# One load of nine tiles in place of a load of two and a load of seven, at the start of a fused LoRA kernel

## The chip, the cores and the metric

The kernel runs on one core of a Trainium2 chip. The metric is device time in microseconds of one execution. A core has a matrix engine (TensorE, "PE" in the profile), a vector engine (VectorE, "DVE"), an activation engine (ScalarE, "ACT"), a general engine (GpSimd, "POOL") and a sequencing engine (SyncE, "SP"). Sixteen DMA engines move data between the chip's memory (HBM) and the on-chip memory (SBUF). The engines run side by side and meet at semaphores. In this kernel every DMA is issued by SP, on one queue.

## The reference

```python
def setup_inputs():
    batch, seq, d_model, r = 16, 512, 768, 16
    # x (16, 512, 768), A (768, 16) * 0.1, B (16, 768) * 0.1, all float32; scale = 0.5

def reference(x, A, B, scale):
    lora = np.matmul(np.matmul(x, A), B)
    return (x + scale * lora).astype(np.float32)
```

So every token, a row of 768 floats, gets a low-rank correction added: y = x A has 16 numbers per token, and out = x + 0.5 y B. There are 16 * 512 = 8192 tokens. x and out are 25.2 MB each.

## The kernel before, in words

**Tiles, parts and groups.** A tile is 128 tokens, one on each SBUF partition, so there are 64 tiles of 128 x 768 floats (384 KB each). The tiles are cut twice, by two different sizes. For the transfers there are five parts of 9, 7, 16, 16 and 16 tiles (`PARTS`); within a part each partition holds that many neighbouring tokens, so a load of n tiles reads one contiguous row of n * 3 KB for each partition. `LOADS` lists the loads as (part, first tile, number of tiles), `STORES` the stores. For the computation there are eight groups of eight tiles (`GROUP`). x stays in SBUF in float32 (`x_all`, called x_sb in the profile), the correction is added in place, and the stores read from there. There is room for 48 tiles. The last part's 16 tiles therefore go where parts 0 and 1 were, and its two loads wait until the stores of these parts are done.

**One group.** Half of the eight tiles are narrowed to float16 (xn) by ScalarE and half by GpSimd (`narrowed`, L194). VectorE transposes them in 32 x 32 blocks (xt, L250). TensorE multiplies them with A, spread out as a block-diagonal weight w_bd, in 24 matmuls (y_ps, L281). ScalarE copies the result, scaled, into the block-diagonal y_bd (four instructions, L238). TensorE multiplies that with B, four pairs of tiles one after another, each pair into one of two halves of PSUM (lora_ps, L302). VectorE adds each pair to x in place (L255). In VectorE's order the transposes of group g + 1 stand ahead of the four additions of group g.

**Group 0 and the weights** have an order of their own. GpSimd clears its buffers, builds `pick`, narrows the first two tiles of x (L194, called with 0, 0, 2), then narrows B (L212) when it has landed, then builds w_bd from A transposed (L214, L220). ScalarE narrows tiles 2 and 3, then 4 to 7. VectorE first transposes A (L243), then the two halves of group 0 (L250). GpSimd's narrowing of the first two tiles and the three loads of A count on the same semaphore, s_a, and VectorE's transpose of A waits for all four. A narrowing waits for the load that its tiles come with: `load_of` looks that up in `LOADS`, so the first narrowing on each engine that needs a load waits for all of that load.

**SP's queue.** The order is written out by hand: load 0, load 1, the three loads of A (after GpSimd has cleared a_rows), the load of B, loads 2 to 5; then, when group 1's additions are done and TensorE has finished the tenth pair of tiles (`s_lora` at 2 * PAIRS + 2), the stores of parts 0 and 1; when each of these has landed, a load of the last part (L139); then the stores of parts 2, 3 and 4 (L149), each after the group that completes it, the first of them not before TensorE has begun the pairs of group 5 (`s_raise` at 6). SP does nothing but issue and wait, and the sixteen DMA engines work their own lists of rows off in the order of issue: each of them gets 8 of the 128 rows of a load or store.

Of the kernel before, what the change touches and what calls it, by code (L numbers as in the profile page):

```python
# [28 lines left out]
def kernel(  # L29
# [66 lines left out]
    def memory(t2, i, s, n):  # L96
        S = PARTS[i]
        return t2[ds(parts[i], S * P), :].rearrange("(p s) d -> p s d", s=S)[:, ds(s, n), :]

    def held(i, s, n):  # L100
        return tiles(where.index((i, s)), n)

    def tiles(t, n):
        return x_all[:, ds(t % ROOM, n), :]

    LOADS = [
        (0, 0, 2), (0, 2, 7), (1, 0, 7), (2, 0, 8), (2, 8, 8), (3, 0, 16), (4, 0, 8), (4, 8, 8)
    ]
    s_load = [sem(f"s_load{k}") for k in range(len(LOADS))]

# [25 lines left out]
    def on_sync(e):  # L136
        def load(k):
            ld = LOADS[k]
            e.dma_start(out=held(*ld), in_=memory(x2, *ld)).then_inc(s_load[k], 16)  # L139

        def summed(k):
            e.wait_ge(s_sum, sorted(set(STORED)).index(STORED[k]) + 1)
            if STORED[k] + 1 < NG:

                e.sem_inc(s_free[PAIRS - 1], 1)

        def store(k, done):
            st = STORES[k]
            e.dma_start(out=memory(out2, *st), in_=held(*st)).then_inc(done, 16)  # L149

        load(0)
        load(1)
        e.wait_ge(s_ready, 1)
        blocks = A.rearrange("(c e) r -> c (e r)", e=64)
        for c in range(SETS):
            e.dma_start(
                out=a_rows[c : SET * SET : SET, :], in_=blocks[ds(c * SET, SET), :]
            ).then_inc(s_a, 16)
        e.wait_ge(s_brows, 1)
        e.dma_start(out=b_rows[0 : R * APART : APART, :], in_=B).then_inc(s_b, 16)  # L160
        for k in range(2, len(LOADS) - 2):
            load(k)

        for p in range(2, PAIRS):
            e.sem_inc(s_free[p], 1)
        summed(0)


        e.wait_ge(s_lora, 2 * PAIRS + 2)
        store(0, s_out0)  # L170
        store(1, s_out1)
        e.wait_ge(s_out0, 16)
        load(len(LOADS) - 2)
        e.wait_ge(s_out1, 16)
        load(len(LOADS) - 1)
        for k in range(2, len(STORES)):
            summed(k)
            if k == 2:


                e.wait_ge(s_raise, 6)
            store(k, s_out)
# [90 lines left out]
    def on_tensor(e):  # L273
# [58 lines left out]
        for p in range(PAIRS):  # L332
            raised(p)

    on_sync(nc.sync)
    on_gpsimd(nc.gpsimd)
    on_scalar(nc.scalar)
# [46 lines left out]
```

## Time and profile before

| | us |
|---|---|
| time, median of 3 runs | 123.75 (123.57 to 123.76) |
| time of the profiled execution | 123.43 |
| its span, first to last instruction | 121.6 |
| busy: VectorE | 81.7 |
| busy: TensorE matmuls | 49.8 |
| busy: ScalarE | 37.4 |
| busy: GpSimd | 28.4 |
| DMA packets' time, share of 16 engines over the span | 97.0% |

The page gives, for the slowest core, each engine's busy time, a strip of 40 slices with a digit for the busy tenths of each, the DMA queues, the chain of work that ended last, the costliest groups of instructions, and the DMA issues. The trace behind it answers with instructions in order of time, with what each waited for. It also has a record of each DMA packet: here one packet is one row of a load or store, with start, length and bytes. "Landing" of a DMA is the moment at which its semaphore has its full count.

### The profile page before, as it was taken

The numbers are of one execution on the slowest core, as the hardware profiler recorded it, in microseconds if no ns is written. First come the engines' busy times: TensorE is split into PE (matmuls) and PEld (weight loads), VectorE is DVE, ScalarE is ACT, GpSimd is POOL, SyncE is SP. The second block draws the span as 40 slices with busy tenths as digits, with TensorE's granted clock in tenths as the row PEclk, the third lists the DMA queues.
The fourth block names the chain that finished last, engine by engine and source line by source line (L and its number), as shares of the span: only waits on it lengthen the run. The fifth ranks groups of instructions, "written<-read, shape, count | busy, mean of one in ns | idle before, by whom it ended". The sixth has DMA issues, their size and how long they took to land.

```text
span 121.6 us, 884 instructions
## 1 busy us (share of the span) xinstructions
PE 49.8 (41%) x322; PEld 29.2 (24%) x322; DVE 81.7 (67%) x42; ACT 37.4 (31%) x43; POOL 28.4 (23%) x24
## 2 busy tenths in 40 slices
PE   0000209487457547746745734774674320000000
PEld 0000006253223424424423322442442110000000
DVE  0000970599999999999999989999995990000000
ACT  4000967626408312735340093643004000000000
POOL 7730567126009002605300080620000000000000
PEclk9999999999999999999999999999999995555555
DMA  3999999999999897999999999998999899899890
GB/s 63 437 431 457 446 398 469 404 420 469 437 517 420 356 517 336 427 421 410 446 416 436 428 428 485 420 517 372 404 517 404 372 517 404 372 517 404 372 517 0
DMA packets 1928, 50.43 MB, mean 415 GB/s; under 512 B 236, under 2 KB 236, under 8 KB 392
## 3 DMA queue, kind: packets, MB, share of 16 engines
q1 hardware_dynamic: 1928, 50.43, 97.0%
HBM read 25.26 MB, written 25.17 MB: 415 GB/s over the span
## 4 chain that ended last, share of the span: by engine, by line
DVE 33%; DMA 29%; PE 9%; ACT 6%; POOL 2%; issue 2%; SPq 0%; DVEq 0%
DVE x_sb L255 21%; DMA x_sb<-in_x_dram 20%; DVE xt L250 12%; DMA out_dram<-x_sb 9%; PE ps_yt L281 6%; ACT xn L194 3%; PE lora_ps L302 3%; ACT y_bd L238 2%; POOL xn L194 2%; SPq L139 0%; SPq L379 0%; DVEq L268 0%; SPq L134 0%
## 5 line engine op out<-in xcount | busy, mean ns | idle before, releaser
L255 DVE TENSOR_TENSOR x_sb<-x_sb,lora_ps 128x1536 f32<-128x1536 f32 x32 | 53.7, 1735 | 1.4 <-PE lora_ps L302 1.4
L194 ACT CAST xn<-x_sb 128x3072 f16<-128x3072 f32 (+1 forms) x9 | 23.4, 2609 | 35.9 <-DMA x_sb<-in_x_dram 24.8
L302 PE MATMUL lora_ps<-b_mm,y_bd 128*128 128x512 f16 (+1 forms) x128 | 25.0, 328 | 22.6 <-ACT y_bd L238 14.3
L194 POOL CAST xn<-x_sb 128x3072 f16<-128x3072 f32 (+1 forms) x8 | 20.7, 2586 | 43.9 <-DMA x_sb<-in_x_dram 24.6
L250 DVE STREAM_TRANSPOSE xt<-xn 128x3072 f32<-128x3072 f32 (+1 forms) x9 | 27.1, 3006 | 5.3 <-PE ps_yt L281 4.4
L281 PE MATMUL ps_yt<-xt,w_bd 128*128 128x256 f16 x192 | 25.2, 282 | 12.2 <-DVE xt L250 12.2
L281 PEld LDWEIGHTS ps_yt<-xt,w_bd 128*128 128x128 f16 x192 | 18.5, 99 | 19.7 <-issue 15.4
L302 PEld LDWEIGHTS lora_ps<-b_mm,y_bd 128*128 128x128 f16 x128 | 10.6, 97 | 35.5 <-ACT y_bd L238 16.6
L238 ACT ACTIVATE y_bd<-ps_yt 32x256 f16<-32x256 f32 x32 | 12.0, 374 | 18.7 <-PE ps_yt L281 18.4
L243 DVE STREAM_TRANSPOSE a_t<-a_rows 32x1024 f32<-32x1024 f32 x1 | 2.0, 1955 | 12.2 <-DMA a_rows<-in_A_dram 12.2
L315 PE MATMUL lora_ps<-b_half,pick 128*128 128x512 f16 (+1 forms) x2 | 0.8, 500 | 13.5 <-POOL b_half L212 13.5
L315 PEld LDWEIGHTS lora_ps<-b_half,pick 128*128 128x128 f16 x2 | 0.1, 105 | 13.5 <-issue 13.5
L212 POOL CAST b_half<-b_rows 128x768 f16<-128x768 f32 x1 | 0.8, 827 | 5.5 <-DMA b_rows<-in_B_dram 5.5
L220 POOL COPY w_bd<-w_one 32x384 f16<-32x384 f16 x4 | 2.0, 500 | 0.2
L194 ACT ACT_TABLE_LOAD x1 | 1.3, 1283 | 0.9 <-SPq L134 0.9
L202 POOL MEMSET w_bd<- 128x1536 f32 x1 | 1.4, 1372 | 0.0
L214 POOL CAST w_one<-a_t 32x384 f16<-32x384 f32 x1 | 0.9, 857 | 0.9 <-DVE a_t L243 0.9
L199 POOL MEMSET a_rows<- 32x1024 f32 x1 | 0.9, 941 | 0.5 <-SPq L134 0.5
L231 ACT CAST b_mm<-lora_ps 128x768 f16<-128x768 f32 x1 | 0.8, 798 | 0.0
L200 POOL MEMSET b_rows<- 128x768 f32 x1 | 0.7, 728 | 0.0
L203 POOL MEMSET y_bd<- 128x512 f32 x1 | 0.5, 514 | 0.0
L205 POOL TENSOR_SCALAR_AFFINE_SELECT pick<-pick 128x128 f16<-128x128 f16 x1 | 0.3, 298 | 0.0
(5 smaller groups left out, 0.6 us busy)
## 6 DMA issues: line engine op xcount, KB each, us to landing
out_dram<-x_sb SPq DMA_DIRECT2D x3, 6144.0 KB, 20.1
x_sb<-in_x_dram SPq DMA_DIRECT2D x4, 3072.0 KB, 17.6
x_sb<-in_x_dram SPq DMA_DIRECT2D x1, 6144.0 KB, 41.6
x_sb<-in_x_dram SPq DMA_DIRECT2D x2, 2688.0 KB, 12.4
out_dram<-x_sb SPq DMA_DIRECT2D x1, 3456.0 KB, 11.5
out_dram<-x_sb SPq DMA_DIRECT2D x1, 2688.0 KB, 17.7
x_sb<-in_x_dram SPq DMA_DIRECT2D x1, 768.0 KB, 4.5
a_rows<-in_A_dram SPq DMA_DIRECT2D x3, 16.0 KB
```

The source lines that it names most:

```text
L194: ins = copy(out=xn[:, ds(first, n), :], in_=tiles(t, n))
L199: e.memset(a_rows[0:Q], 0.0).then_inc(s_ready, 1)
L202: e.memset(w_bd.rearrange("p c k m -> p (c k m)").bitcast(fp32), 0.0)
L214: e.tensor_copy(out=w_one.rearrange("i (c e) k r -> i c e (k r)", c=SETS), in_=a_t[0:Q].rearrange("i k r (e c) -> i c e (k r)", c=SET)[:, ...
L220: e.tensor_copy(out=w_bd[ds(b * Q, Q), :, :, ds(b * Q, R)], in_=w_one).then_inc(s_w, 1)
L238: last = e.mul(out=y_bd[q, :, q], in_=y_ps[q, :, :], mul=sc)
L243: e.transpose(out=a_t[0:Q].rearrange("i k r c -> i (k r) c"), in_=a_rows[0:Q].rearrange("c (i k r) -> c (k r) i", k=2, r=R),).then_inc(s_r ...
L250: return e.transpose(out=ts[0], in_=ts[1])
L255: ins = e.tensor_tensor(out=xs, in0=xs, in1=lora[p % 2], op=mybir.AluOpType.add)
L281: mm = e.matmul(y_ps, w_bd[:, c, k, :], xv[:, :, c, :, k], start=(m == 0), stop=(m == MMS - 1),)
L302: mms.append(e.matmul(t[:, k, ds(n0, w)], y_bd[:, 2 * p + k, :], b_mm[:, ds(n0, w)], start=True, stop=True,))
L315: last = e.matmul(lora[0][:, 0, ds(n0, w)], pick.rearrange("p b r -> p (b r)"), b_half[:, ds(n0, w)], start=True, stop=True,)
```

## The change

The first nine tiles of x are one part in memory. They came as two loads, one of tiles 0 and 1 (rows of 6 KB) and one of tiles 2 to 8 (rows of 21 KB). Now they come as one load of nine tiles with rows of 27 KB, and SP issues one DMA fewer. The later loads keep their place in SP's order, with numbers one lower. The narrowings look up their load in the list: GpSimd's narrowing of tiles 0 and 1 now waits for the load of nine tiles, as ScalarE's of tiles 2 and 3 does (before, that waited for the load of seven). No instruction of the other engines is added, removed or reordered.

```diff
     LOADS = [
-        (0, 0, 2), (0, 2, 7), (1, 0, 7), (2, 0, 8), (2, 8, 8), (3, 0, 16), (4, 0, 8), (4, 8, 8)
+        (0, 0, 9), (1, 0, 7), (2, 0, 8), (2, 8, 8), (3, 0, 16), (4, 0, 8), (4, 8, 8)
     ]
...
         load(0)
-        load(1)
         e.wait_ge(s_ready, 1)
...
-        for k in range(2, len(LOADS) - 2):
+        for k in range(1, len(LOADS) - 2):
             load(k)
```

## The prediction

> **What bounds the kernel now.** I read the page's strip and queue table first, to see which resource is full, then the busy time by stretches, then the instructions of the start in order of time, then the chain up to the first store.
>
> ```profile
> span 121.6 us, 884 instructions
> ...
> DMA  3999999999999897999999999998999899899890
> ...
> q1 hardware_dynamic: 1928, 50.43, 97.0%
> ```
>
> No compute engine is over 67%, but the sixteen DMA engines are busy 97% of the span: 50.43 MB, nearly all of it x in and out. The strip dips only around slices 13 to 15, where loads give way to stores. So I cut the span there:
>
> ```profile
> core 0: us, PE busy (x) PEld busy (x) DVE busy (x) ACT busy (x) POOL busy (x), PEclk, DMA share, GB/s
> 1.97:12.10 10.13, 0.00 (x0) 0.00 (x0) 0.00 (x0) 0.22 (x1) 4.29 (x6) 1.00 1.04 414
> 12.10:44.45 32.35, 18.44 (x114) 10.84 (x114) 27.33 (x14) 17.67 (x18) 11.92 (x9) 1.00 1.01 432
> 44.45:46.45 2.00, 0.58 (x6) 0.53 (x7) 2.00 (x2) 0.00 (x0) 0.00 (x0) 1.00 0.91 393
> 46.45:47.30 0.85, 0.85 (x9) 0.55 (x6) 0.85 (x2) 0.00 (x0) 0.00 (x0) 1.00 1.22 521
> 47.30:62.50 15.20, 8.99 (x61) 5.31 (x60) 15.20 (x10) 8.27 (x10) 5.49 (x2) 1.00 1.00 427
> ...
> 77.00:120.25 43.25, 12.64 (x82) 6.91 (x79) 22.24 (x13) 5.73 (x9) 2.75 (x1) 0.76 0.97 418
> ```
>
> The last but one column is the DMA share (packets are counted by their start, so a short stretch can read over or under 1). It stays at 1: 0.91 and 1.22 together make up 1.00 over 44.45 to 47.30. The packet records say it row by row: from the first row at 1.98 to the last row's end at 120.22, no engine pauses by 0.05 us between two rows. The kernel therefore ends when the DMA engines have worked off a fixed list of rows. A change moves the time if it makes the list shorter, or lets an engine run out of rows before SP issues the next.
>
> The start, in order of time:
>
> ```profile
> 5.57 1.46 POOL L194 CAST xn<-x_sb 128x1536 f16<-128x1536 f32 x1 [0.73 <-DMA x_sb<-in_x_dram]
> 12.12 4.13 ACT L194 CAST xn<-x_sb 128x1536 f16<-128x1536 f32 x2 [9.93 <-DMA x_sb<-in_x_dram]
> 12.23 1.96 DVE L243 STREAM_TRANSPOSE a_t<-a_rows 32x1024 f32<-32x1024 f32 x1 [12.23 <-DMA a_rows<-in_A_dram]
> 12.52 0.83 POOL L212 CAST b_half<-b_rows 128x768 f16<-128x768 f32 x1 [5.49 <-DMA b_rows<-in_B_dram]
> ...
> 14.12 1.72 DVE L250 STREAM_TRANSPOSE xt<-xn 128x1536 f32<-128x1536 f32 x1
> 14.25 0.86 POOL L214 CAST w_one<-a_t 32x384 f16<-32x384 f32 x1 [0.90 <-DVE a_t L243]
> 15.17 2.18 POOL L220 COPY w_bd<-w_one 32x384 f16<-32x384 f16 x4
> 16.27 0.80 ACT L231 CAST b_mm<-lora_ps 128x768 f16<-128x768 f32 x1
> 16.28 1.78 DVE L250 STREAM_TRANSPOSE xt<-xn 128x1536 f32<-128x1536 f32 x1 [0.44 <-ACT xn L194]
> 18.18 0.77 PEld L281 LDWEIGHTS ps_yt<-xt,w_bd 128*128 128x128 f16 x5 [4.57 <-issue]
> 18.21 1.01 PE L281 MATMUL ps_yt<-xt,w_bd 128*128 128x256 f16 x4 [3.92 <-DVE xt L250]
> ```
>
> GpSimd narrows its two tiles at 5.57, long before anything else can go on. At 12.1 the load of seven, A and B land nearly together, and then VectorE, GpSimd and ScalarE each have a queue of work before TensorE can begin at 18.21. And the chain to the first store:
>
> ```profile
> 42.95 1.49 PE lora_ps L302 x8
> 44.44 0.02 issue
> 44.45 11.48 DMA out_dram<-x_sb
> ```
>
> The first store is issued at 44.45, when TensorE's tenth pair is done. VectorE has no idle time between its transpose at 22.51 and that moment (52.28, 42.36, 32.44, 22.51: a period of 9.92 us), so a delay of group 0 arrives at the store undiminished.
>
> **The change, part by part.** The sum is made against the profiled execution: span 121.6, execution 123.43, so 1.83 around the span; the median of the runs, 123.75, is 0.32 above it, and I move it by the same difference.
>
> *Rows.* Each engine had eight rows of 6 KB and eight of 21 KB; now eight of 27 KB. In the packet records a 6 KB row takes 0.234 us when the stream runs, a 21 KB row 0.799, and a row of 27,648 bytes (part 0's store; rows of 48 KB take the same time in loads and stores) 1.025. So 8 * (0.234 + 0.799 - 1.025) = 0.06 us less per engine. The first rows are slower: the 128 small rows average 0.318, hence 8 * 0.084 = 0.67 us of start-up per engine. Bounds: all of it stays (0), or all goes (-0.67). Nearly all of it sits on each engine's first row or two, which looks like the wait for the first bytes, and a large first row waits for those too. I take 0.
>
> *SP.* One DMA issue less, 0.42 us. The loads of A are issued at 1.92 because they wait for GpSimd's clearing (0.95 + 0.94), so nothing behind them moves.
>
> *The narrowing on GpSimd.* It leaves the idle time at 5.57 and goes to the landing of the nine tiles, taken as 12.10 as before (the list ahead of it is only 0.06 shorter). It runs 12.14 to 13.60. Behind it on GpSimd wait B's narrowing (12.52, now 13.6 to 14.45) and w_one. VectorE's transpose of A waits for it by s_a: 12.23 becomes 13.7 (with 0.1 between engines, as from 72.46 to 72.57 later), ending at 15.67. The first half of group 0 follows at 15.6, the second at 17.25 instead of 16.28: the 0.44 us for which VectorE waited there is used up. w_one starts at 15.72, w_bd is done at 18.8 (17.35 before), before the second half (19.05), so GpSimd isn't last. B's path reaches ScalarE at 15.5, before it is free at 16.26. TensorE begins at 19.15 to 19.2: group 0 is 0.95 us later. Bounds: 0.5, if the nine tiles land sooner (the engine that landed last before had 1.27 us of start-up against a mean of 0.67); 1.0, if they don't and every handover costs 0.1.
>
> *What hides it.* The first store would be issued at 45.40. How long from issue to first row? In the empty queue of the start 1.01 (0.97 to 1.98); for part 2's store at most 1.23 (74.47 to 75.70, with no pause). So its rows are ready at 46.41 to 46.63. The engines run out of loads between 46.47 and 47.29, less 0.06. For the first engine the cover was 0.8 to 1.0 us, and what is left is 0 or -0.2. Five engines run out at 46.41 to 46.49 and may pause by up to 0.2, five at 46.59 to 46.67 by less than 0.05, and the other six, from 46.83 on, have 0.2 to 0.8 to spare. So the price is 0 to 0.2 on a few engines. I take 0: the engines that run out last here are mostly those that finish last at the end.
>
> *Later.* The chain to part 2's store hangs on the landing of the last part's first load (69.66) and ScalarE's narrowing until 72.43; group 5's projection, over at 71.08, may come 1.3 us later before it counts. VectorE idles 0.38 us at 72.2, so its delay shrinks to 0.6. The last store, issued at 100.97, is needed when the store before it runs out, near 104.7 (75.7 + 16 * 1.815). All of that covers 0.95 us.
>
> Sum: -0.06 + 0 + 0 = -0.06. Span 121.54, execution 123.37, median 123.7.
>
> **The rivals.** *Slower: the first store comes too late.* The cover at 46.4 is used up, and TensorE's own pace at the start is uncertain:
>
> ```profile
> 18.21 3.26 PE L281 MATMUL ps_yt<-xt,w_bd 128*128 128x256 f16 x15 [3.92 <-DVE xt L250]
> ```
>
> Fifteen matmuls take 3.26 us (0.217 each); later twelve take 1.50 (0.125). The granted clock reads 1.00 in both stretches. If the slow stretch lasted through all 24, they would take 5.2 instead of 4.26: 0.95 more, which before was just covered and now comes on top. Then the store is issued at 46.35, its rows are ready at 47.4 to 47.6, and every engine pauses, the last to run out by 0.1 to 0.4, the first by 1.0 to 1.2; an engine that has run dry may pay start-up again (up to 0.67). That gives +0.3 to +1.0: 124.0 to 124.7, 124.2 in the middle. It decides from a delay of 1.0 us on (first engine) and fully from 1.8 (last). For it: there is no cover left by my own sum. Against it: it needs both delays at once.
>
> [...]
>
> *Faster: the start-up goes with the small rows.* If fewer, larger rows spare the engines their second late row (two or three of the sixteen have one, 0.3 to 0.5 us) and part of the first, the list ends 0.3 to 0.6 sooner: 123.1 to 123.4. Against it: the first row is late on fifteen of sixteen engines, whatever follows.
>
> *Faster: every DMA costs the queue a fixed time.* The only such time in the rows lies between the last row of the load of seven (end 11.54) and its landing (12.10): 0.56 us. If the queue stood still for it, one load fewer would give 123.1. Against it: the first row of the load of seven starts at 4.43, where the last small row ends. The chance is 0.01.
>
> [...]
>
> **How the numbers follow.** Within 0.2% (0.25 us, about what a measurement of this kernel can tell from no change): 0.50, the forecast. Slower: 0.31, the late store. Faster: 0.19, of it 0.18 the start-up. The range goes from half of the faster rival (123.3) to a little over the middle of the slower (124.3).
>
> **What would show it.** Right: GpSimd's first narrowing near 12.1, A's transpose near 13.7, TensorE's start near 19.1, the first store's issue near 45.4, a DMA share of 1 across 44 to 48, rows of 27 KB at 1.02 us. Wrong: a pause of the DMA engines before the first store's rows, a TensorE start past 19.5, or first rows much shorter or longer than before.

## The result and the profile after

| | before | after |
|---|---|---|
| median, us (six runs each) | 123.66 (123.47 to 123.76) | 124.65 (124.22 to 124.94) |
| ratio after / before, 95% interval | | 1.0076 (1.0059 to 1.0092) |
| profiled execution, us | 123.43 | 124.94 |
| its span, us | 121.6 | 123.1 |

The change makes the kernel slower by 0.8%, about 1 us. The forecast was 123.7 and the range went up to 124.3; the rival that ended on the slower side, a first store that comes too late, is what happened, near the top of its price (124.0 to 124.7). A second measurement of the changed kernel gave 1.0072 (1.0050 to 1.0095), with single executions from 123.50 to 125.22. The kernel before stays within 123.3 to 124.0 in nearly all of its runs: the change did not only add time, it made the time uneven.

The page of the changed kernel, with the same three lines as before:

```profile
span 123.1 us, 883 instructions
...
DMA  5999999999999896999989999997997998999790
...
q1 hardware_dynamic: 1784, 50.43, 96.4%
```

There are 144 packets fewer and the same bytes. The share of the span went down from 97.0% to 96.4%: the DMA engines lost time. Where, the stretches around the first store show (last column but one: DMA share):

```profile
12.38:44.45 32.07, 17.98 (x106) 10.53 (x106) 25.06 (x13) 17.08 (x17) 13.31 (x10) 1.00 1.01 435
44.45:46.45 2.00, 1.35 (x8) 0.70 (x8) 2.00 (x2) 0.59 (x2) 0.00 (x0) 1.00 0.91 393
46.45:47.40 0.95, 0.13 (x1) 0.00 (x0) 0.95 (x1) 0.00 (x0) 0.00 (x0) 1.00 0.01 0
47.40:62.50 15.10, 9.62 (x67) 5.92 (x68) 15.10 (x9) 7.00 (x6) 5.49 (x2) 1.00 1.02 417
```

From 46.45 to 47.40 no row begins at all: 0 GB/s. The last rows of the loads run out between 46.46 and 47.51, and the first rows of the store begin between 47.45 and 47.60. Before, every engine went from one to the other without a pause of 0.05 us. The start of the changed kernel, in order of time (start, duration, engine, line, operation, tile written and tile read, and in brackets the idle time before and what ended it), tells why:

```profile
12.40 4.12 ACT L193 CAST xn<-x_sb 128x1536 f16<-128x1536 f32 x2 [10.21 <-DMA x_sb<-in_x_dram]
12.44 1.46 POOL L193 CAST xn<-x_sb 128x1536 f16<-128x1536 f32 x1 [7.60 <-DMA x_sb<-in_x_dram]
13.84 0.83 POOL L211 CAST b_half<-b_rows 128x768 f16<-128x768 f32 x1
13.93 1.95 DVE L242 STREAM_TRANSPOSE a_t<-a_rows 32x1024 f32<-32x1024 f32 x1 [13.93 <-POOL xn L193]
...
15.82 3.38 DVE L249 STREAM_TRANSPOSE xt<-xn 128x1536 f32<-128x1536 f32 x2
...
19.35 5.28 PE L280 MATMUL ps_yt<-xt,w_bd 128*128 128x256 f16 x24 [3.74 <-DVE xt L249]
...
46.61 0.35 SPq L149 DMA_DIRECT2D out_dram<-x_sb  x1
```

GpSimd's narrowing of the first two tiles now starts at 12.44 instead of 5.57, VectorE's transpose of A waits for it (the releaser in its brackets is now POOL xn, before it was A's load), and TensorE begins at 19.35 instead of 18.21. Then comes a second delay that the change did not make: the 24 matmuls take 5.28 us instead of 4.26. Together group 0 ends 2.15 us later, and the first store is issued 2.16 later, at 46.61.

**The account of the lost time.** In the packet records I took, for each row, its duration above the duration of such a row in the running stream, and averaged over the sixteen engines. Pauses ahead of the first store's rows: 0.62 us. Slow rows between 59 and 64.5, where part 1's store gives way to the next load: 0.78, against 0.18 before, so 0.60 more. Start-up (rows that begin before 12 us): 0.81 against 0.68, so 0.13 more. All other rows: 0.13 more. The sum is 1.48. From it goes the 0.06 by which the rows of 27 KB are shorter in the running stream, so an engine should end 1.42 later. In the mean over the engines the last row ends 1.43 later (121.10 against 119.67), and on the engine that ends last 1.52 later (121.74 against 120.22); the spans differ by 1.5.

### The profile page after: what moved, and what is told of

Its sections match the earlier page's. It is cut to its first block, busy times and chain, and to the rows that moved or that the text cites. A ratio compares the mean times of both kernels' runs of the same rounds, so it can differ in the third digit from the quotient of the medians.

```text
span 123.1 us, 883 instructions
## 1 busy us (share of the span) xinstructions
PE 52.1 (42%) x322; PEld 30.2 (25%) x322; DVE 81.5 (66%) x42; ACT 37.4 (30%) x43; POOL 28.3 (23%) x24
## 3 DMA queue, kind: packets, MB, share of 16 engines
q1 hardware_dynamic: 1784, 50.43, 96.4%
## 4 chain that ended last, share of the span: by engine, by line
DVE 61%; DMA 9%; PE 7%; issue 3%; ACT 1%; POOL 1%; SPq 0%
DVE x_sb L254 37%; DVE xt L249 22%; DMA x_sb<-in_x_dram 9%; PE ps_yt L280 5%; DVE a_t L242 2%; PE lora_ps L301 1%; ACT y_bd L237 1%; POOL xn L193 1%; SPq L378 0%; SPq L134 0%
## 5 line engine op out<-in xcount | busy, mean ns | idle before, releaser
L301 PE MATMUL lora_ps<-b_mm,y_bd 128*128 128x512 f16 (+1 forms) x128 | 25.7, 334 | 21.2 <-ACT y_bd L237 13.5
L280 PE MATMUL ps_yt<-xt,w_bd 128*128 128x256 f16 x192 | 27.0, 294 | 11.7 <-DVE xt L249 11.7
L280 PEld LDWEIGHTS ps_yt<-xt,w_bd 128*128 128x128 f16 x192 | 19.3, 103 | 20.3 <-issue 15.2
```

The source lines that it names most:

```text
L280: mm = e.matmul(y_ps, w_bd[:, c, k, :], xv[:, :, c, :, k], start=(m == 0), stop=(m == MMS - 1),)
L301: mms.append(e.matmul(t[:, k, ds(n0, w)], y_bd[:, 2 * p + k, :], b_mm[:, ds(n0, w)], start=True, stop=True,))
```

## The experiments

All profiles' numbers for the first store are in one table, in order of its issue. "Pause" and "slow rows" are means over the sixteen engines from the packet records as above; the slow rows are given around the change from loads to stores (43 to 47.5) and from part 1's store to the next load (59 to 64.5).

| kernel | 24 matmuls: start, us they take | first store issued | pause | slow rows 43-47.5 | slow rows 59-64.5 | span |
|---|---|---|---|---|---|---|
| before, store earlier | 18.04, 4.82 | 42.93 | 0 | 0.62 | 0.02 | 122.2 |
| after, both repairs | 18.37, 2.84 | 43.72 | 0 | 0.46 | 0.02 | 121.9 |
| before, loads of 7 and 2 | 17.51, 4.64 | 44.13 | 0 | 0.06 | 0.04 | 121.8 |
| after, store earlier | 19.28, 4.80 | 44.14 | 0 | 0.12 | 0.11 | 122.1 |
| after, A's transpose free | 18.23, 4.11 | 44.32 | 0 | 0.04 | 0.18 | 121.6 |
| before | 18.21, 4.26 | 44.45 | 0 | 0.01 | 0.18 | 121.6 |
| after, TensorE kept busy | 19.18, 2.83 | 44.53 | 0 | 0.02 | 0.12 | 121.8 |
| before, wait only, second profile | 18.62, 4.30 | 44.91 | 0 | 0.02 | 0.29 | 122.1 |
| before, wait only | 18.78, 4.26 | 45.02 | 0 | 0.01 | 0.25 | 121.7 |
| before, wait only, third profile | 18.91, 4.31 | 45.20 | 0 | 0.01 | 0.35 | 121.8 |
| after, second profile | 19.11, 4.25 | 45.35 | 0 | 0.01 | 0.32 | 121.9 |
| after, third profile | 19.07, 4.52 | 45.58 | 0 | 0.01 | 0.54 | 122.3 |
| after | 19.35, 5.28 | 46.61 | 0.62 | 0.02 | 0.78 | 123.1 |
| before, wait and more | 20.19, 5.07 | 47.24 | 1.31 | 0.01 | 0.86 | 123.8 |
| before, store later | 17.82, 4.21 | 47.84 | 1.91 | 0.01 | 0.82 | 124.4 |

**1. The wait without the load of nine.** The two loads stay; GpSimd waits for both:

```diff
         ).then_inc(s_pick, 1)
+        e.wait_ge(s_load[1], 16)
         narrowed(e, e.tensor_copy, 0, 0, SUB // 2)
```

> The two loads of the kernel before stay; GpSimd's first narrowing waits for the load of seven as well. Theory (the wait delays group 0, so the first store comes too late and the DMA engines pause): GpSimd narrows at 12.1 to 12.4, VectorE's transpose of A starts at 13.7 to 13.9, TensorE's first group at 19.1 to 19.4, the first store is issued at 45.4 to 46.6, and the time is that of the changed kernel, 124.2 to 124.9. Rival (the rows of 27 KB or the common start of one large load cost the DMA engines time by themselves): as the kernel before, 123.5 to 123.8.

Measured: 124.22 in the median of twelve, ratio 1.0039 (1.0017 to 1.0060). Four executions lie at 123.46 to 123.63, as the kernel before, and eight at 124.18 to 124.55. The profile is of the quickest of them:

```profile
18.78 4.26 PE L282 MATMUL ps_yt<-xt,w_bd 128*128 128x256 f16 x24 [3.73 <-DVE xt L251]
...
45.02 0.82 SPq L149 DMA_DIRECT2D out_dram<-x_sb  x2
```

TensorE starts 0.57 later than before, the store is issued 0.57 later, its rows are still ready in time. So the wait alone costs time, but only in some executions, and about half of what the change costs. The start is earlier than in the changed kernel because the load of seven landed at 11.8 here, the load of nine at 12.4. That is no accident of two profiles: by the start of ScalarE's narrowing, the seven profiles with loads of two and seven have the load of seven at 11.7 to 12.1, the seven with the load of nine have that at 12.1 to 12.4. So the load of nine adds about 0.35 us of its own to a wait that is there.

Two more profiles were meant to catch a slower execution.

> The kernel before with only the wait for the load of seven, profiled once more: of its twelve timed executions four were at 123.5 to 123.6 and eight at 124.2 to 124.6, and the profile came from the quick group. Theory: in an execution of the slower group TensorE's first 24 matmuls take 4.8 to 5.3 in place of 4.26, the first store is issued at 45.6 to 46.3, and the DMA engines pause ahead of it by 0.1 to 0.9; in one of the quicker group 24 matmuls take under 4.6 and nothing pauses. Rival (the slower group has another cause): a slower execution without pauses, or pauses with a quick group of matmuls.

> The same kernel a third time, as which group an execution falls into is left to chance (two in three for the slower). Theory and rival as for the second profile.

They gave 123.87 and 123.58, both with short matmuls (4.30 and 4.31) and no pause. That agrees with the theory as far as it goes, but no profile shows a slower execution of this kernel.

The record of the twelve timed executions has the span and the mean granted clock of each. The four quick ones have spans of 121.7 to 121.8 and a mean clock of 0.912 to 0.914, the eight slower ones 122.4 to 122.7 and 0.888 to 0.906. The mean does not tell when in an execution the clock was low: the kernel before, in the same comparison, reads 0.885 to 0.914 at spans of 121.5 to 122.2 (and 0.692 at 122.8, once). So that the slower executions are those in which TensorE's first matmuls are slow, and that the DMA engines pause in them, is inferred from the other kernels' profiles; no run of this kernel shows it.

**2. The load of nine without the wait on VectorE.** In the changed kernel the narrowing of two tiles counts on a semaphore of its own:

```diff
+    s_two = sem("s_two")
...
-        ins.then_inc(s_narrow if g else s_first if first else s_a, 1)
+        ins.then_inc(s_narrow if g else s_first if first else s_two, 1)
...
-        e.wait_ge(s_a, SETS * 16 + 1)
+        e.wait_ge(s_a, SETS * 16)
...
+        e.wait_ge(s_two, 1)
         for h in range(2):
             e.wait_ge(s_first, h + 1)
```

> The changed kernel with its one load of nine, but VectorE's transpose of A no longer waits for GpSimd's narrowing: the narrowing has a semaphore of its own, and only the transpose of group 0's first half waits for it. Theory: the transpose of A starts at about 12.5 when A lands, w_bd is done at about 17.8, TensorE starts near 18.5, the first store is issued by 45.7, no or short pauses of the DMA engines, 123.5 to 123.9. Rival: the load is what costs, so as the changed kernel, 124.2 to 124.9.

Measured: 123.86, ratio 1.0025 (1.0004 to 1.0045), twelve runs. The median span is 121.8, that of the kernel before in the same comparison; the remaining 0.26 lies outside the span (see the last section). In order of time:

```profile
18.23 4.11 PE L282 MATMUL ps_yt<-xt,w_bd 128*128 128x256 f16 x24 [2.87 <-DVE xt L250]
...
44.32 0.82 SPq L150 DMA_DIRECT2D out_dram<-x_sb  x2
```

TensorE starts when it did before, and nothing pauses. So the load of nine costs nothing in the span once nobody on the path waits for GpSimd's narrowing.

**3. An earlier first store,** in the changed kernel and, as a control, in the kernel before:

```diff
-        e.wait_ge(s_lora, 2 * PAIRS + 2)
+        e.wait_ge(s_lora, 2 * PAIRS)
```

> The changed kernel, with the first store two pairs of tiles earlier in TensorE's order (s_lora at 2 * PAIRS, not + 2), so that only group 1's additions hold it up. Theory: TensorE's first group stays late (19.3, over at 23.6 to 24.7), the first store is issued at 43.5 to 44.7 in place of 46.6, its rows are ready before the loads run out, no pause, 123.5 to 123.8. Rival: the front or the load costs by itself, so as the changed kernel, 124.2 to 124.9, with no pause to be seen but slow rows elsewhere.

> The kernel before with the same earlier first store. Theory: the store is issued at about 42.5 in place of 44.45, and as no engine paused there, nothing changes: 123.5 to 123.8. If an earlier store gains or costs by itself (rows written beside rows read), this run shows it, up to 0.5 either way, and the run with the changed kernel has to be read against it.

Measured: 123.81 for the changed kernel, ratio 1.0008 (0.9991 to 1.0026), and 124.03 for the kernel before, ratio 1.0030 (1.0011 to 1.0050). The changed kernel with the earlier store, in order of time:

```profile
19.28 4.80 PE L280 MATMUL ps_yt<-xt,w_bd 128*128 128x256 f16 x24 [3.75 <-DVE xt L249]
...
44.14 0.82 SPq L149 DMA_DIRECT2D out_dram<-x_sb  x2
```

Group 0 is as late as expected and takes 4.80, and most of the loss is gone all the same, as the store is issued at 44.14. So the front's delay has little price of its own. The kernel before with the earlier store:

```profile
18.04 4.82 PE L281 MATMUL ps_yt<-xt,w_bd 128*128 128x256 f16 x24 [3.87 <-DVE xt L250]
...
42.93 0.82 SPq L149 DMA_DIRECT2D out_dram<-x_sb  x2
```

Here the edit costs 0.4 us, which the expectation had only as a side case: the store goes out four microseconds ahead of its turn, and the last rows of the loads are slow by 0.62 us per engine. The store can come too early, too.

**4. TensorE kept busy ahead of group 0.** The changed kernel, with eight matmuls whose result nothing reads:

```diff
         last.then_inc(s_bp, 1)
+        for k in range(8):
+            e.matmul(
+                lora[1][:, k % 2, ds(0, 512) if k % 2 == 0 else ds(256, 512)],
+                pick.rearrange("p b r -> p (b r)"), b_half[:, ds(0, 512)], start=True, stop=True,
+            )
```

> The changed kernel with eight extra matmuls of 512 columns on TensorE between the spreading of B and group 0, into PSUM that nothing reads; they fill its idle time from 15.6 to 19.0. The wait on GpSimd and the load of nine stay. Theory (half of the delay is TensorE's slow stretch, which ends by time and not by a number of matmuls): group 0 still starts at 19.3 but its 24 matmuls take 3.0 to 3.7 in place of 5.3, the first store is issued at 44.4 to 45.1 in place of 46.6, no pause, 123.5 to 123.8, and the runs lie within 0.4 of each other. Rival (the start delay of 1.1 is enough by itself): 24 matmuls faster, but pauses stay and the time is 124.2 or more.

Measured: 124.15, ratio 1.0057 (1.0034 to 1.0080): by the time, the rival. By the trace, the theory:

```profile
15.24 3.10 PE L320 MATMUL lora_ps<-b_half,pick 128*128 128x512 f16 x8
...
19.18 2.83 PE L280 MATMUL ps_yt<-xt,w_bd 128*128 128x256 f16 x24 [0.85 <-DVE xt L249]
...
44.53 0.82 SPq L149 DMA_DIRECT2D out_dram<-x_sb  x2
```

The start is as late as in the changed kernel, the granted clock's first change to full speed comes at 17.67, ahead of group 0, the 24 matmuls take 2.83, the store is issued at 44.53, nothing pauses, and all twelve spans lie at 121.6 to 122.1, as the kernel before (121.6 to 122.1 in 23 runs). The half microsecond that is left lies outside the span: 1.96 to 3.45 us there, 1.76 to 1.86 in the kernel before. The expected time was missed by what lies outside the span, and all loads and stores lie inside it.

**5. The price of a late store by itself.** The kernel before with the store one pair of tiles later:

```diff
-        e.wait_ge(s_lora, 2 * PAIRS + 2)
+        e.wait_ge(s_lora, 2 * PAIRS + 3)
```

> The kernel before, its front untouched, with the first store one pair of tiles later in TensorE's order (s_lora at 2 * PAIRS + 3): the price of a late store by itself. Theory: issued at about 48.3 in place of 44.45, rows ready at 49.2, the engines pause 1.9 to 2.7 each (2.35 in the mean); 125.6 to 126.1 if the pause is all, 126.1 to 126.6 if the slow rows near 61.4 of the changed kernel follow from the engines' common start after a pause. Rival (DMA engines catch up later): under 125.

Measured: 126.52, ratio 1.0251 (1.0214 to 1.0287), in four executions from 126.01 to 127.33. The profile is of one of 126.18; the two longer ones (126.86 and 127.33, spans 125.1 and 125.6) it doesn't explain. Its stretches (columns as before):

```profile
46.55:48.65 2.10, 1.20 (x8) 0.41 (x6) 2.10 (x3) 0.93 (x1) 0.90 (x1) 1.00 0.00 0
48.65:63.50 14.85, 8.93 (x60) 5.31 (x60) 14.85 (x8) 7.56 (x10) 4.59 (x2) 1.00 1.04 424
```

The store is issued at 47.84, its first row begins at 48.68, the engines pause by 1.91 in the mean, and the slow rows near 62 come as in the changed kernel: 0.82 against 0.18. From the pause (1.91), the slow rows (0.64 more) and the rest (0.19 more) one gets 2.74; the last row ends 2.76 later than before (122.98 against 120.22). Nothing is caught up later.

**6. Large first rows without a delay.** The two loads, cut as seven and two:

```diff
-        (0, 0, 2), (0, 2, 7), (1, 0, 7), (2, 0, 8), (2, 8, 8), (3, 0, 16), (4, 0, 8), (4, 8, 8)
+        (0, 0, 7), (0, 7, 2), (1, 0, 7), (2, 0, 8), (2, 8, 8), (3, 0, 16), (4, 0, 8), (4, 8, 8)
```

> The kernel before with its first two loads of seven and two tiles in place of two and seven: large rows at the start, and the first tiles wait for a load three times as large, but it still lands ahead of A. Theory: GpSimd narrows at about 9.6 to 11.1, which nothing waits for; TensorE starts at 17.5 to 18.3, the first store is issued at 43.7 to 45.2, no pause, 123.4 to 123.8. Rival (large first rows cost by themselves): 124.0 or more.

Measured: 123.56, ratio 0.9994 (0.9985 to 1.0002), 123.43 to 123.73 over twelve runs. GpSimd narrows at 10.23 to 11.69, still ahead of A's landing, and TensorE starts at 17.51. So a first load of seven tiles costs nothing here: what matters is whether it lands before A or with it.

**7. Both repairs at once** (2 and 4 together).

> The changed kernel with both repairs: the transpose of A no longer waits for GpSimd's narrowing, and the eight extra matmuls keep TensorE busy up to group 0. Theory: TensorE starts at about 18.2 to 19.1, 24 matmuls in 3.0 to 3.9, the first store at 43.5 to 44.6, no pause; the time is that of the kernel before or 0.1 less (rows 0.06), 123.4 to 123.7. Rival (the load of nine costs by itself): 123.9 or more.

Measured: 124.19, ratio 1.0045 (1.0032 to 1.0058), five executions, with a median span of 121.8, the same as before. Here too the time lies outside the span (2.38 to 2.49). The store comes out early, at 43.72, with 0.46 us of slow rows at the end of the loads.

**8. The delay made larger, with the two loads of before.** GpSimd waits for the load of seven and narrows the two tiles once more, into a buffer that nothing reads:

```diff
+    spare = sb("spare", [P, 2, D], MM_DT)
...
+        e.wait_ge(s_load[1], 16)
+        e.tensor_copy(out=spare, in_=tiles(0, 2))
         narrowed(e, e.tensor_copy, 0, 0, SUB // 2)
```

> The kernel before with its two loads, with GpSimd's wait for the load of seven, and with one more narrowing of the two tiles into a buffer that nothing reads (1.46 us more on GpSimd): a delay of about 2.0 us at the start without the load of nine, whatever TensorE's slow stretch does. Theory: TensorE starts at 20.0 to 20.4, the first store is issued at 45.9 to 47.5, its rows begin 0.84 later, the engines that run out at 46.4 pause by 0.3 to 1.9, near 62 their rows are slow by 0.4 to 0.8, every execution is slower than the kernel before, 124.2 to 125.8, and pauses and slow rows add up to the difference of the spans within 0.3. Rival (it takes the load of nine to lose the time): 123.5 to 124.0.

Measured: 125.52, ratio 1.0139 (1.0108 to 1.0169), each of the four executions slower (124.64 to 125.78). In order of time, and the stretch ahead of the store's first rows:

```profile
20.19 5.07 PE L284 MATMUL ps_yt<-xt,w_bd 128*128 128x256 f16 x24 [3.73 <-DVE xt L253]
...
47.24 0.82 SPq L150 DMA_DIRECT2D out_dram<-x_sb  x2
```

```profile
46.45:48.05 1.60, 0.76 (x5) 0.24 (x3) 1.60 (x1) 0.00 (x0) 0.00 (x0) 1.00 0.01 0
```

The pause is 1.31, the slow rows are 0.86. Pause, additional slow rows (0.68) and the rest add up to 2.0; the spans differ by 2.2. A delay of this size loses the time without the load of nine.

**9. The changed kernel, twice more.**

> The changed kernel profiled once more, as a second point on the line from the time of the first store's issue to the pauses. Theory: TensorE starts at 19.1 to 19.5 and takes 4.1 to 5.3 for 24 matmuls; the store's rows begin 0.84 after its issue or when an engine runs out of loads, whichever is later; the span follows from that as in the first profile. Rival: the span doesn't follow the issue.

> The changed kernel unchanged, in twelve timed executions and one more profile. Theory (the length of TensorE's slow stretch is drawn anew in each execution and decides between pause and none): executions spread from 123.6 to 125.0, a minority of them under 123.9, the profile's store issue and pause agreeing with its 24 matmuls (4.2 to 4.4 us: issue at 45.2 to 45.5 and no pause; 5.3 us: 46.4 to 46.7 and 0.4 to 0.7 in the mean). Rival (the first six executions were slow for a reason of that chip alone): nearly all under 123.9.

The second profile belongs to an execution of 123.69:

```profile
19.11 4.25 PE L280 MATMUL ps_yt<-xt,w_bd 128*128 128x256 f16 x24 [3.74 <-DVE xt L249]
...
45.35 0.82 SPq L149 DMA_DIRECT2D out_dram<-x_sb  x2
```

TensorE starts nearly where it did in the first profile (19.35), but its matmuls take 4.25, and then nothing pauses. Timed again, twelve executions gave 123.50 to 125.22, median 124.59, two of them under 123.9. The third profile, of an execution of 124.12, lies between:

```profile
19.07 4.52 PE L280 MATMUL ps_yt<-xt,w_bd 128*128 128x256 f16 x24 [3.75 <-DVE xt L249]
...
45.58 0.83 SPq L149 DMA_DIRECT2D out_dram<-x_sb  x2
```

The store is issued just in time, nothing pauses, but there are 0.54 us of slow rows, which the expectation did not have.

The mean granted clock does not order the eighteen timed executions of the changed kernel: the two quickest, 123.50 and 123.84, have 0.912, the other sixteen, 124.08 to 125.22, have 0.879 to 0.914. So only its three profiles tie a slow execution to slow first matmuls (4.25 us of them at 123.69, 4.52 at 124.12, 5.28 at 124.94).

## Why the prediction was wrong

**The DMA engines as the bound:** right. In the three kernels for which the account was made, the engines' pauses and slow rows add up to the lost span within 0.2 us. These are means, and the span goes by the last engine: in the other profiles the last engine's last row ends up to 0.4 us later than the mean tells (most in the second profile of the wait only).

**Rows (-0.06):** wrong in sign, and small. The rows' own time is less, as computed, but the first 27 KB row of an engine takes 1.76 us where a 6 KB row took 0.78: it pays 0.73 above its running time, the small one 0.55. Start-up is 0.68 to 0.82 with the load of nine, 0.59 to 0.73 in the profiles that kept the two loads of two and seven. Nothing of it went away.

**The narrowing (group 0 starts 0.95 later, bounds 0.5 to 1.0):** right in mechanism, a little short in size: 1.14 in the first profile, 0.90 and 0.86 in the others. The load of nine landed at 12.4, where 12.1 was taken, and at 12.1 to 12.2 in the later two. That the load of nine lands about 0.35 later than the load of seven (experiment 1) was not in the sum.

**The first store (issued at 45.40, rows ready 1.01 to 1.23 later, price 0):** this is the step that failed. In it I carried the 4.26 us of TensorE's 24 matmuls over from the profile before as if it belonged to the work. It does not: it is one draw, and 4.26 was a quick one; the profiles without extra matmuls have 4.11 to 5.28. In the second profile of the changed kernel the draw happened to be 4.25, and there this step holds: issue at 45.35, no pause. That its time, 123.69, is also the forecast's is luck in part, as its start-up is 0.13 and its slow rows near 61 are 0.14 above those before, which the sum did not have. With 5.28 the store is issued at 46.61, 0.84 later its rows are ready, and the engines have run dry. The rival had this mechanism, but took both delays at once for the rarer case (0.31); of the nineteen executions of the changed kernel sixteen were over 123.9. The kernel before has the same uncertainty (4.21 to 4.82 in the three profiles whose front is untouched), but its cover hid it. That cover was larger than I took it to be: where the engines stood waiting, a store's rows began 0.84 after its issue (46.61 to 47.45, 47.84 to 48.68) and not 1.01 to 1.23, so the first engine had 1.2 us to spare and not 0.8 to 1.0. The change used nearly all of it up, which the prediction said; that a cover of nearly zero has a price of zero was the mistake.

The draw goes with the trace's record of the granted clock. In the profiles before and after the change this has entries of 1.00 and 0.50, and the first is a change to full speed, 1.00: at 21.24 in the kernel before, where the fifteen matmuls begun ahead of it take 3.26 us (0.217 each) and the twelve at 26.03 take 1.50 (0.125 each). In the thirteen profiles without extra matmuls this first change comes 2.7 to 5.4 us after the start of group 0 on TensorE: 3.03 after it in the kernel before, 5.41 in the changed one, 3.02 in its second profile. It does not come at a fixed time after the start: in the three profiles of the changed kernel TensorE starts at 19.35, 19.11 and 19.07, and the change comes at 24.76, 22.13 and 22.66. The changes that follow lie 78.51 us behind it in the kernel before, and 51.20, 3.41 and 23.89 us one behind the other in the changed one; what places them was not shown. The matmuls' time follows the delay: 4.11 at 2.71 us, 4.26 at 3.03, 4.52 at 3.59, 4.80 at 4.16, 5.07 at 4.71, 5.28 at 5.41, where all 24 ran ahead of the change. The strip of the page could not show this: it reads 9 before the first entry, too, and I took that 1.00 as a measured full clock.

**The price of a late store (0.3 to 1.0, in the rival):** the pauses were sized right for an engine (0 to 1.15 in the first profile), but not what follows. Start-up was not paid again there: between 43 and 47.5 the slow rows are 0.02, and between 47.4 and 59 they are 0.12. But behind the pause all sixteen engines start together (47.45 to 47.60), and they reach the last row of part 1's store together (61.33 to 61.63, where the kernel before has 60.24 to 61.03); the rows there cost another 0.60. That they follow from the late store is shown by the late store alone, which brings them in the kernel before (0.82 against 0.18).

**Later steps:** right. The wait for part 2's store and the last store stayed covered: in the second profile part 2's store is issued at 74.50 (74.47 in the kernel before). The 100.97 of the last store is the end of its issue; it begins at 100.6.

## What to carry to other kernels

When the transfers bound a kernel and a change takes cover away from an issue, compare what is left not with zero but with how much the chain ahead of that issue varies from execution to execution. A duration taken from one profile is one draw; in this kernel TensorE's first 24 matmuls after idling are a place where the draw changes by a microsecond (4.11 to 5.28 us). The small first load earned its place here not by its bytes but by letting a side job, on which something later waited, be done before everything else lands at once.

## What the runs showed that I had not expected

**A store can be queued too early.** When the first store goes out at 42.9 to 43.7, its rows wait behind the loads, and the last rows of the loads take 0.46 to 0.62 us longer per engine; at 44.1 to 45.6 this is 0.12 or less. At the other turn, near 61, the opposite: slow rows grow from 0.02 to 0.86 as the store's issue moves from 42.9 to 47.2. Their sum is least (0.10 to 0.23) between 44.1 and 44.5, where the kernel before had put it. Why a row is slow at such a turn was not tried, and an engines' common start is not needed for it: the changed kernel's third profile has 0.54 near 61 without a pause.

**Time outside the span.** The kernels with eight more matmuls have the span of the kernel before and still take 0.4 to 0.6 us more: 1.96 to 3.45 and 2.38 to 2.49 us around the span, where the kernels before and after have 1.75 to 1.86. The kernel with one more semaphore on GpSimd's narrowing has both: six executions at 1.89 to 1.95, six at 2.26 to 2.31. Where this time is spent the profile does not show, and it stays open.
